# Hybrid encoder layer: the filters' sums of squares and the Hyena column weights on VectorE, the filters' sum one step later, and a final norm that is shared between ScalarE and VectorE

## The chip, the cores and the metric

The kernel runs on one core of one Trainium2 chip. A core has five engines that matter here, each of which works through its own list of instructions in order: TensorE (PE in the profile) multiplies matrices, VectorE (DVE) and ScalarE (ACT) work on tiles element by element, GpSimd (POOL) can do a part of what VectorE does, and SyncE (SP) issues the DMAs. Where an instruction needs what another engine makes, it waits, and all that is behind it on its engine waits too.

The metric is the device time of one execution in microseconds (us). A kernel is judged by the median of several runs.

## What is computed

One layer of a bidirectional encoder over 1024 positions of width 1024, in float32:

```python
x = x + 0.5 * _swiglu(_rmsnorm(x, ffn1_norm), ffn1_w_gu, ffn1_w_down)
h = _rmsnorm(x, mix_norm)
u_hy, u_rw, g_hy, g_rw = jnp.split(h @ w_in, split_at, axis=-1)
y_hy = _hyena_branch(u_hy, ...)
y_rw = _rwkv7_branch(u_rw, ...)
merged = jax.nn.sigmoid(g_hy) * y_hy + jax.nn.sigmoid(g_rw) * y_rw
x = x + merged @ w_out
x = x + 0.5 * _swiglu(_rmsnorm(x, ffn2_norm), ffn2_w_gu, ffn2_w_down)
return _rmsnorm(x, final_norm)
```

Two parts of it matter for the change. The Hyena branch makes its long filters from a small network, scales every filter by its own length, and takes the spectrum of it:

```python
k = jnp.concatenate([fwd, zero, jnp.flip(bwd[1:], axis=0)], axis=0)
k = k * lax.rsqrt(jnp.sum(k * k, axis=0, keepdims=True) + FILTER_EPS)
```

and the last step of the layer is a norm with one weight per feature:

```python
y = xf * lax.rsqrt(jnp.mean(xf * xf, axis=-1, keepdims=True) + RMS_EPS)
return (y * g.astype(jnp.float32)).astype(x.dtype)
```

## The kernel before

**Matmuls.** Every large product is made in three passes: each operand is split into a coarse part (`hi`, a cast, line 33) and the rest (`lo`, a subtraction, line 37), and `mm3` (lines 43 to 45) adds hi·hi, lo·hi and hi·lo in PSUM. Weights come by DMA into a staging tile `w_st`, ScalarE casts `w_hi`, and a second engine subtracts to get `w_lo`. `col_weights` does this for a column block of 128 features; its argument `lo_eng` names the engine of the subtraction, and without it that is GpSimd.

**Stages.** The first FFN, the mixer, the second FFN and the final norm follow each other. A tile framework with a scheduler sets the order of the instructions on each engine ahead of time, by its own estimate of when each is ready; at run time that order is fixed. So an edit at one place can move rows at others.

**The Hyena columns (some 786 to 1066 us).** The loop over `order` (lines 1324 to 1356) takes 12 column blocks of `w_in`. For each, `half` makes two halves of the product (PE, tile `pw`), `ShortConv.take` copies them into `sh_u` and `sh_o` on ScalarE (lines 545 and 546), and `ShortConv.finish` adds the two outer taps of a width-3 convolution with two VectorE instructions of 128x1024 (line 552), transposes the block in eight small matmuls (`hy_tp`, line 558), copies it on ScalarE (`sh_x`, line 559) and stores it.

Between the blocks the loop advances a generator `bg`, `hyena_filters`, which makes four filters. Each filter takes eight taps: a matmul `ps_h` (line 420), an exponential `ex` (422) and a square `sq` (432) on ScalarE, a product `kt` (424) and an even and an odd sum `eo` (438, 440) on VectorE, and on GpSimd the running sum `acc` of the squares (433; the first of the eight is written by ScalarE at line 428, so seven sums are left). After the eighth tap `ac2` (line 499; the trace calls it `ac`) folds `acc`, two sets of small matmuls (501 and 506) add it over the partitions, and a chain over VectorE and ScalarE (503 to 513) makes the scales. Those scales also multiply the convolution's weights `cw` (line 1349). Then `ps_k` (line 448) is the last product of the spectrum, and lines 458 to 525 put its parts together and store them (`kout`). `bg` gives control back at each `yield`, twelve times in a filter; the loop takes it to step 3i before block i, and to the end of the filter that a block needs.

Each engine's list mixes these two kinds of work, the blocks and the filters. PE waits where neither has anything ready.

**After it** the long convolutions run (from about 1066 us), with the next columns of `w_in` beside them: there VectorE already makes the `w_lo` tiles itself (line 1246).

**The end.** In the last group of the second FFN, `down` adds a block of 128 features and 512 positions to `xT` (line 226), `down_weights` makes that block's weights through a chain DMA, ScalarE, GpSimd (tiles `wdst`, `wd_hi`, `wd_lo`), and `Norm.add` squares the block on ScalarE and sums it on VectorE (lines 92 and 93). When the eight blocks of a half (t = 0 or 1) are done, `finish` makes 1/rms and, for each of four row tiles and two halves j of the features, transposes `xT` on PE (`f_ps`, line 1764), scales it on VectorE with the row's 1/rms and with `grow`, a copy of the final norm's weights in all partitions (line 1767), and stores 256 KB (line 1769).

Of the kernel before, what the change touches and what calls it, by code (L numbers as in the profile page):

```python
# [20 lines left out]
P = 128  # L21
# [135 lines left out]
def bcast_row(ap, n=P):  # L157

    return bass.AP(tensor=ap.tensor, offset=ap.offset, ap=[[0, n]] + [list(d) for d in ap.ap])
# [226 lines left out]
def hyena_filters(tc, ctx, I, K, h2, k_dram, scl):  # L386
# [16 lines left out]
    for o in range(2):  # L403
        for hb in range(NHB):
# [13 lines left out]
            def taps(r):  # L418
                ps = psh.tile([P, 2, HB], F32, name="ps_h", tag="ps_h")
                nc.tensor.matmul(ps, h2[:, r, :], w3b, start=True, stop=True)  # L420
                ex = two.tile([P, 2, HB], F32, name="ex")
                nc.scalar.activation(ex, dec, AF.Exp, scale=tneg[:, r : r + 1])
                kt = two.tile([P, 2, HB], F32, name="kt")
                nc.vector.tensor_tensor(kt, ps, ex, ALU.mult)
                if r == 0:
                    nc.vector.memset(kt[0:1, 1, :], 0.0)
                if first[0]:
                    nc.scalar.activation(acc, kt, AF.Square)
                    first[0] = False
                else:  # L430
                    sq = two.tile([P, 2, HB], F32, name="sq")
                    nc.scalar.activation(sq, kt, AF.Square)
                    nc.gpsimd.tensor_tensor(acc, acc, sq, ALU.add)
                return kt

            def even_odd(r, kt):
# [60 lines left out]
            yield  # L497
            ac2 = two.tile([P, HB], F32, name="ac2", bufs=1)
            nc.vector.tensor_tensor(ac2, acc[:, 0], acc[:, 1], ALU.add)
            ps = psh.tile([P, 512], F32, name="ps_h", tag="ps_h")  # L500
            nc.tensor.matmul(ps[0:1, 0:HB], ones, ac2, start=True, stop=True)
            srow = two.tile([1, HB], F32, name="srow", bufs=1)
# [710 lines left out]
def mixer_in(tc, I, K, ident, wp, pw, hl, scl, h2, h2ctx, dr):  # L1213
# [3 lines left out]
    with ExitStack() as ctx:  # L1217
# [100 lines left out]
        with ExitStack() as c2:  # L1318
# [2 lines left out]
            cw = K.cw  # L1321

            order = (8, 9, 10, 11, 0, 1, 2, 3, 4, 5, 6, 7)
            weights = lambda t: col_weights(nc, wp, I["w_in"][:, ts(t, P)], KD)

            w = {t: weights(t) for t in order[0:3]}
            conv = lambda t: ShortConv(nc, two, sx, ptp, ident, cw[:, t])
# [296 lines left out]
def hybrid_layer_kernel(ctx: ExitStack, tc: tile.TileContext, I: dict, out: bass.AP):  # L1624
# [29 lines left out]
    with tc.tile_pool(name="hB", bufs=1) as hp, tc.tile_pool(name="mip", bufs=3, space=PSUM) as pw:  # L1654
# [3 lines left out]
        with ExitStack() as c2:  # L1658
# [3 lines left out]
            with ExitStack() as c3:  # L1662
# [4 lines left out]
                def done(d, t):  # L1667
                    nc.sync.dma_start(x_dram[:, d, ts(t, 512)], xT[:, d, ts(t, 512)])
                    nm.add(xT[:, d, ts(t, 512)], t)
# [58 lines left out]
    with ExitStack() as ctx2:  # L1728
# [20 lines left out]
        with ExitStack() as c3:  # L1749
# [1 line left out]
            pmm = c3.enter_context(tc.tile_pool(name="ffbp", bufs=2, space=PSUM))  # L1751
            nf = Norm(nc, np_, npp, ident, live["ones"], K.norm["final_norm"], "nm2")

            grow = c3.enter_context(tc.tile_pool(name="fg", bufs=1)).tile([P, D], F32, name="f_g")
            nc.sync.dma_start(grow, bcast_row(I["final_norm"]))

            def finish(t):
                r = nf.rstd(t)
                for q in range(4):
                    i = 4 * t + q  # L1760
                    for j in range(KD // 4):
                        ps = pmm.tile([P, 4, P], F32, name="f_ps", tag="pgu", bufs=4)
                        for c in range(4):
                            nc.tensor.transpose(ps[:, c, :], xT[:, 4 * j + c, ts(i, P)], ident)
                        o = np_.tile([P, 512], F32, name="f_o", tag="nm_h") if j else \
                            wp.tile([P, 512], F32, name="f_o", tag="w_st")
                        nc.vector.scalar_tensor_tensor(o, ps.rearrange("p a b -> p (a b)"), r[:, q : q + 1],  # L1767
                                                       grow[:, ts(j, 512)], ALU.mult, ALU.mult)
                        nc.sync.dma_start(out[0, ts(ORDER[i], P), ts(j, 512)], o)

            def pools():
                return (c3.enter_context(tc.tile_pool(name="ffb2", bufs=2)), dn, pmm,
                        lambda: pmm.tile([P, 512], F32, name="pgu", tag="pgu", bufs=4))

            for _ in ffn(nc, pools, wp, xT, live["hl"], I["ffn2_w_gu"], I["ffn2_w_down"],
                         lambda d, t: nf.add(xT[:, d, ts(t, 512)], t), finish):
                pass


# [21 lines left out]
```

## Time and profile before

| | |
|---|---|
| median of 3 runs | 2882.93 us (2874.61 to 2890.05) |
| the profiled execution | 2875.99 us |
| its span | 2874.2 us |
| mean granted clock of TensorE | 0.97 |
| busy: PE, DVE, ACT, POOL | 95%, 43%, 31%, 19% |

The span is the time from the first to the last instruction of the profiled execution; what lies around it is 1.8 us. The profile gives for each engine the busy time, for groups of instructions the mean duration, and for idle time what ended it. A row of the timeline reads: start, duration, engine, line, operation, output and inputs, and in brackets how long the engine had been idle and what released it. The granted clock is the share of full speed that TensorE was allowed to run at.

### The profile page before, as it was taken

To read this page: it belongs to the slowest core of one execution; us is meant where nothing else is said; L and a number is where in the kernel's file an instruction comes from. 1 tells how busy PE (TensorE), PEld (TensorE's weight loads), DVE (VectorE), ACT (ScalarE), POOL (GpSimd) and SP (SyncE) were. 2 spreads that over 40 slices of the span, in tenths; PEclk is the share of its full clock that TensorE was granted. 3 is DMA by queue.
4 is the path that set the end of the run, shared out by engine and by line. 5 is a ranking of instruction groups with operands and counts; after the bars stand their busy time and mean duration, and the time that the engine had idled before them with its cause. 6 is when DMAs were issued, how large, how long until landed. Compare 5 with 4: busy or idle time off the path is not lost. (4 is left out here: it accounts for less than half of the span.)

```text
span 2874.2 us, 46016 instructions
## 1 busy us (share of the span) xinstructions
PE 2723.9 (95%) x19440; PEld 2194.6 (76%) x19440; DVE 1231.8 (43%) x2140; ACT 905.2 (31%) x1515; POOL 550.0 (19%) x351
## 2 busy tenths in 40 slices
PE   8999999999988899989899999898999999999998
PEld 6888888888665667777787877776778888888787
DVE  4111010111647668998765667757541111101114
ACT  5111111111444442334654545532331111111112
POOL 2323233232413210000000000000033232322322
PEclk9999999999988999999999999898999999999999
DMA  5111111111341235553644325457531111111102
GB/s 126 55 48 48 41 55 48 41 52 43 107 148 63 77 127 186 164 169 114 188 118 152 103 88 180 144 171 231 166 88 52 44 52 44 52 44 48 47 27 92
DMA packets 406477, 276.43 MB, mean 96 GB/s; under 512 B 50899, under 2 KB 366879, under 8 KB 405632
## 3 DMA queue, kind: packets, MB, share of 16 engines
q1 hardware_dynamic: 406272, 273.50, 31.5%
q8 instruction: 153, 2.51, 0.4%
q14 instruction: 52, 0.43, 0.0%
HBM read 202.53 MB, written 70.91 MB: 95 GB/s over the span
## 5 line engine op out<-in xcount | busy, mean ns | idle before, releaser
L45 PE MATMUL pw<-hThi,w_lo 128*128 128x512 f32 (+1 forms) x1184 | 472.3, 400 | 15.6 <-DVE w_lo L1246 15.6
L43 PE MATMUL pw<-hThi,w_hi 128*128 128x512 f32 (+1 forms) x1184 | 473.8, 400 | 8.5 <-ACT sh_o L1268 4.4
L44 PE MATMUL pw<-hTlo,w_hi 128*128 128x512 f32 (+1 forms) x1184 | 472.1, 399 | 0.0
L33 ACT CAST w_hi<-w_st 128x1024 fp32r<-128x1024 f32 (+1 forms) x176 | 170.8, 972 | 496.0 <-PE pw L44 187.0
L37 POOL TENSOR_TENSOR w_lo<-w_st,w_hi 128x1024 fp32r<-128x1024 f32 x100 | 240.5, 2405 | 412.3 <-ACT w_hi L33 406.1
L43 PE MATMUL pgu<-hThi,w_hi 128*128 128x512 f32 x704 | 279.0, 396 | 0.8 <-issue 0.8
L44 PE MATMUL pgu<-hTlo,w_hi 128*128 128x512 f32 x704 | 279.1, 396 | 0.2 <-POOL hTlo L37 0.2
L45 PE MATMUL pgu<-hThi,w_lo 128*128 128x512 f32 x704 | 279.1, 397 | 0.0
L43 PE MATMUL pdn<-g_hi,wd_hi 128*128 128x512 f32 x704 | 275.0, 391 | 1.9 <-DVE xT L226 1.9
L44 PE MATMUL pdn<-g_lo,wd_hi 128*128 128x512 f32 x704 | 274.8, 390 | 2.0 <-POOL g_lo L37 2.0
L45 PE MATMUL pdn<-g_hi,wd_lo 128*128 128x512 f32 x704 | 275.0, 391 | 1.4 <-POOL wd_lo L37 1.4
L45 PEld LDWEIGHTS pw<-hThi,w_lo 128*128 128x128 f32 (+1 forms) x1184 | 223.2, 189 | 69.6 <-DVE w_lo L1246 17.8
L43 PEld LDWEIGHTS pw<-hThi,w_hi 128*128 128x128 f32 (+1 forms) x1184 | 223.6, 189 | 63.9 <-ACT sh_o L1268 6.2
L226 DVE SCALAR_TENSOR_TENSOR xT<-pdn,xT 128x512 f32<-128x512 f32 x192 | 132.3, 690 | 314.8 <-PE pdn L45 314.8
L44 PEld LDWEIGHTS pw<-hTlo,w_hi 128*128 128x128 f32 (+1 forms) x1184 | 223.3, 189 | 54.6 <-issue 4.4
L209 DVE TENSOR_TENSOR silu<-silu,pgu 128x512 f32<-128x512 f32 x44 | 30.2, 687 | 449.5 <-PE pgu L45 449.5
L209 DVE TENSOR_TENSOR silu<-silu,pw 128x512 f32<-128x512 f32 x44 | 30.2, 687 | 445.9 <-PE pw L45 445.1
L37 POOL TENSOR_TENSOR wd_lo<-wdst,wd_hi 128x512 fp32r<-128x512 f32 (+1 forms) x112 | 132.4, 1183 | 333.6 <-ACT wd_hi L33 333.6
L37 POOL TENSOR_TENSOR g_lo<-silu,g_hi 128x512 fp32r<-128x512 f32 x88 | 113.5, 1289 | 398.4 <-ACT g_hi L33 398.4
L33 ACT CAST wd_hi<-wdst 128x512 fp32r<-128x512 f32 (+1 forms) x112 | 64.5, 576 | 379.5 <-PE pdn L44 366.9
L37 POOL TENSOR_TENSOR hTlo<-nm_h,hThi 128x512 fp32r<-128x512 f32 x16 | 23.2, 1447 | 740.2 <-ACT hThi L33 740.2
L43 PEld LDWEIGHTS pgu<-hThi,w_hi 128*128 128x128 f32 x704 | 132.5, 188 | 33.2 <-issue 1.2
(316 smaller groups left out, 4461.6 us busy)
## 6 DMA issues: line engine op xcount, KB each, us to landing
w_st<-in_ffn_w_gu SPq DMA_DIRECT2D x88, 512.0 KB, 3.7
w_st<-in_w_in SPq DMA_DIRECT2D x57, 512.0 KB, 3.8
wdst<-in_ffn_w_down SPq DMA_DIRECT2D x64, 256.0 KB, 2.8
wdst<-in_ffn_w_down SPq DMA_DIRECT2D x48, 192.0 KB, 2.5
d_kf<-kout SPq DMA_DIRECT2D x32, 256.0 KB, 2.3
hy_k<-d_kf SPq DMA_DIRECT2D x32, 256.0 KB, 3.3
w_st<-in_w_out SPq DMA_DIRECT2D x16, 512.0 KB, 3.9
d_X<-sh_x SPq DMA_DIRECT2D x12, 512.0 KB, 3.5
```

Source lines behind the costliest of these rows:

```text
L33: nc.scalar.copy(hi, src)
L37: eng.tensor_tensor(lo, src, hi.bitcast(F32), ALU.subtract)
L43: te.matmul(out, lhs[0], rhs[0], start=first, stop=False)
L44: te.matmul(out, lhs[0], rhs[1], start=False, stop=False)
L45: te.matmul(out, lhs[1], rhs[0], start=False, stop=last)
L209: nc.vector.tensor_tensor(sl, sl, pu, ALU.mult)
L226: nc.vector.scalar_tensor_tensor(xa, ps, 0.5, xa, ALU.mult, ALU.add)
```

## The change

Four edits. The sum `acc` of the filters' squares moves from GpSimd to VectorE. A `yield` is put between `ac2` and the matmul that reads it. The `w_lo` tiles of the twelve Hyena column blocks move from GpSimd to VectorE. The final norm's weights are multiplied onto `xT` in place, by ScalarE, as soon as a block has been squared (`done`); the copy of the weights in all partitions goes; the last scaling is left with the row's 1/rms alone, on VectorE for the first half of the features and on ScalarE for the second; and the two halves go into one tile and one store of 512 KB.

```diff
@@ hyena_filters
-                    nc.gpsimd.tensor_tensor(acc, acc, sq, ALU.add)
+                    nc.vector.tensor_tensor(acc, acc, sq, ALU.add)
...
             nc.vector.tensor_tensor(ac2, acc[:, 0], acc[:, 1], ALU.add)
+            yield
             ps = psh.tile([P, 512], F32, name="ps_h", tag="ps_h")
             nc.tensor.matmul(ps[0:1, 0:HB], ones, ac2, start=True, stop=True)
@@ the Hyena columns
-            weights = lambda t: col_weights(nc, wp, I["w_in"][:, ts(t, P)], KD)
+            weights = lambda t: col_weights(nc, wp, I["w_in"][:, ts(t, P)], KD, lo_eng="dve")
@@ the final norm
-            grow = c3.enter_context(tc.tile_pool(name="fg", bufs=1)).tile([P, D], F32, name="f_g")
-            nc.sync.dma_start(grow, bcast_row(I["final_norm"]))
+            fo = c3.enter_context(tc.tile_pool(name="fo", bufs=2))
+
+            def done(d, t):
+
+                x = xT[:, d, ts(t, 512)]
+                nf.add(x, t)
+                nc.scalar.activation(x, x, AF.Copy, scale=nf.g[:, d : d + 1])
 
             def finish(t):
                 r = nf.rstd(t)
                 for q in range(4):
                     i = 4 * t + q
+                    o = fo.tile([P, D], F32, name="f_o") if q % 2 else wp.tile([P, D], F32, name="f_w", tag="w_st")
                     for j in range(KD // 4):
                         ps = pmm.tile([P, 4, P], F32, name="f_ps", tag="pgu", bufs=4)
                         for c in range(4):
                             nc.tensor.transpose(ps[:, c, :], xT[:, 4 * j + c, ts(i, P)], ident)
-                        o = np_.tile([P, 512], F32, name="f_o", tag="nm_h") if j else \
-                            wp.tile([P, 512], F32, name="f_o", tag="w_st")
-                        nc.vector.scalar_tensor_tensor(o, ps.rearrange("p a b -> p (a b)"), r[:, q : q + 1],
-                                                       grow[:, ts(j, 512)], ALU.mult, ALU.mult)
-                        nc.sync.dma_start(out[0, ts(ORDER[i], P), ts(j, 512)], o)
+                        flat = ps.rearrange("p a b -> p (a b)")
+                        if j:
+                            nc.scalar.activation(o[:, ts(j, 512)], flat, AF.Copy, scale=r[:, q : q + 1])
+                        else:
+                            nc.vector.tensor_scalar(o[:, ts(j, 512)], flat, r[:, q : q + 1], None, ALU.mult)
+                    nc.sync.dma_start(out[0, ts(ORDER[i], P), :], o)
...
             for _ in ffn(nc, pools, wp, xT, live["hl"], I["ffn2_w_gu"], I["ffn2_w_down"],
-                         lambda d, t: nf.add(xT[:, d, ts(t, 512)], t), finish):
+                         done, finish):
                 pass
```

The scheduler turns this into new orders. Three places are shown. The first is VectorE's list at the end of the second filter, the last two taps up to `ac`; before:

```order
L424 TENSOR_TENSOR kt<-ps_h,ex 128x512
L438 TENSOR_TENSOR eo<-kt 128x256
L440 TENSOR_TENSOR eo<-kt 128x256
L463 SCALAR_TENSOR_TENSOR cxt<-cxt,ps_k 128x512 x2
L409 SCALAR_TENSOR_TENSOR dec<-dec 128x512
L424 TENSOR_TENSOR kt<-ps_h,ex 128x512
L426 MEMSET kt 1x256
L499 TENSOR_TENSOR ac_5911<-acc 128x256
```

The same place after:

```order
L424 TENSOR_TENSOR kt<-ps_h,ex 128x512
L438 TENSOR_TENSOR eo<-kt 128x256
L440 TENSOR_TENSOR eo<-kt 128x256
L433 TENSOR_TENSOR acc<-acc,sq 128x512
L463 SCALAR_TENSOR_TENSOR cxt<-cxt,ps_k 128x512 x2
L409 SCALAR_TENSOR_TENSOR dec<-dec 128x512
L424 TENSOR_TENSOR kt<-ps_h,ex 128x512
L426 MEMSET kt 1x256
L433 TENSOR_TENSOR acc<-acc,sq 128x512
L499 TENSOR_TENSOR ac_5911<-acc 128x256
```

Each tap has one row more, `acc`, behind its `eo` rows, and it needs the square that ScalarE makes of the same `kt`; GpSimd's list loses those rows, and the `w_lo` rows of the blocks.

The second place is PE's list at the transposes of the second block (`hy_tp`), which wait for the line 552 pair; `pw` rows belong to the next block, `L376` to the small network of the filters. Before:

```order
L43 MATMUL pw<-hThi_119,w_hi 128x512
L376 MATMUL ps_h<-feats,w_5082 64x512
L558 MATMUL hy_tp<-ident,sh_o 128x128 x8
L44 MATMUL pw<-hTlo_120,w_hi 128x512
L45 MATMUL pw<-hThi_119,w_lo 128x512
```

After (the lines behind the new `yield` count one more, so line 558 is 559):

```order
L43 MATMUL pw<-hThi_119,w_hi 128x512
L376 MATMUL ps_h<-feats,w_5082 64x512
L44 MATMUL pw<-hTlo_120,w_hi 128x512
L45 MATMUL pw<-hThi_119,w_lo 128x512
L43 MATMUL pw<-hThi_119,w_hi 128x512
L44 MATMUL pw<-hTlo_120,w_hi 128x512
L45 MATMUL pw<-hThi_119,w_lo 128x512
L559 MATMUL hy_tp<-ident,sh_o 128x128 x8
```

Five `pw` matmuls have moved ahead of the transposes.

The third place is ScalarE's list in the second half (t = 1) of the last FFN group; the blocks of features are counted from 0 to 7. The `CAST` rows make the blocks' weights, the line 92 rows are the squares. Before, from the cast of block 3 on, which the square of block 1 follows:

```order
L33 CAST wd_hi<-wdst 128x384
L92 ACTIVATE nm_sq<-xT 128x512
L33 CAST wd_hi<-wdst 128x384 x2
L92 ACTIVATE nm_sq<-xT 128x512 x2
L33 CAST wd_hi<-wdst 128x384
L92 ACTIVATE nm_sq<-xT 128x512
L33 CAST wd_hi<-wdst 128x384
L92 ACTIVATE nm_sq<-xT 128x512 x3
```

After, from the cast of block 4 on, which the square of block 2 follows:

```order
L33 CAST wd_hi<-wdst 128x384
L92 ACTIVATE nm_sq<-xT 128x512
L1761 ACTIVATE xT<-xT,k_final_norm 128x512
L92 ACTIVATE nm_sq<-xT 128x512
L1761 ACTIVATE xT<-xT,k_final_norm 128x512
L92 ACTIVATE nm_sq<-xT 128x512
L33 CAST wd_hi<-wdst 128x384
L1761 ACTIVATE xT<-xT,k_final_norm 128x512
L33 CAST wd_hi<-wdst 128x384 x2
L92 ACTIVATE nm_sq<-xT 128x512
```

The cast of block 5 stood ahead of the squares of the blocks 2 and 3 before; after, it stands behind the squares of the blocks 2, 3 and 4.

## The prediction

> **What bounds the kernel now.** I read the page first: the busy times, then the forty slices of 72 us for PE and for its granted clock.
>
> ```profile
> PE 2723.9 (95%) x19440; PEld 2194.6 (76%) x19440; DVE 1231.8 (43%) x2140; ACT 905.2 (31%) x1515; POOL 550.0 (19%) x351
> PE   8999999999988899989899999898999999999998
> PEclk9999999999988999999999999898999999999999
> ```
>
> PE is the bound nearly everywhere; what another engine saves pays only where PE waits for it. Slices 11 to 14 show 8s, in the clock too. The table by stage shows what that is (columns: window, length, then the busy time and the instructions of PE, PEld, DVE, ACT and POOL, the granted clock, DMA share, GB/s).
>
> ```profile
> 800.00:850.00 50.00, 41.13 (x165) 30.42 (x165) 29.48 (x38) 24.45 (x34) 10.53 (x4) 0.90 0.28 83
> 900.00:950.00 50.00, 42.11 (x177) 32.06 (x177) 39.33 (x68) 23.00 (x35) 14.56 (x8) 0.93 0.29 93
> 1200.00:1400.00 200.00, 182.38 (x887) 143.90 (x886) 178.11 (x265) 80.24 (x131) 0.96 (x1) 0.98 0.53 157
> 2200.00:2820.00 620.00, 618.98 (x2679) 502.66 (x2678) 80.23 (x117) 102.87 (x148) 178.51 (x111) 1.00 0.15 44
> 2820.00:2874.20 54.20, 44.42 (x223) 36.50 (x221) 34.57 (x59) 19.61 (x34) 15.43 (x15) 0.92 0.36 122
> ```
>
> The second FFN has no room: PE fills 619 of 620 us. The Hyena columns lose 8 to 9 of 50 us, and the end loses 10 of 54. PE's waits between 786 and 1066 us (sum, times, longest):
>
> ```profile
> PE hy_tp L558 <- DVE sh_o L552: 17.3, 10, 3.6
> PE ps_h L501 <- DVE ac L499: 6.9, 4, 4.4
> PE hy_tp L558 <- DVE sh_u L539: 3.6, 1, 3.6
> ```
>
> Of these 27.8 us, 17.3 are the transposes' wait for VectorE's line 552 pair; the longest single wait, 4.4 us, is the first filter's fold waiting for the last sum.
>
> **Why VectorE is late there.** GpSimd does the sums and the `w_lo` tiles, and the two engines stretch each other. The groups of this stage:
>
> ```profile
> L433 POOL TENSOR_TENSOR acc<-acc,sq 128x512 f32<-128x512 f32 x28 | 41.0, 1463 | 97.7 <-ACT sq L432 97.7
> L37 POOL TENSOR_TENSOR w_lo<-w_st,w_hi 128x1024 fp32r<-128x1024 f32 x9 | 22.5, 2499 | 85.3 <-ACT w_hi L33 79.1 <-PE ps_k L448 6.1
> L458 DVE TENSOR_TENSOR cxt<-cxt,ps_k 128x512 f32<-128x512 f32 x16 | 10.0, 678 | 1.4 <-PE ps_k L448 1.4
> L1246 DVE TENSOR_TENSOR w_lo<-w_st,w_hi 128x1024 fp32r<-128x1024 f32 x3 | 3.7, 1220 | 1.6 <-ACT w_hi L1245 1.6
> L552 DVE SCALAR_TENSOR_TENSOR sh_o<-sh_u,k_cw,sh_o 128x1024 f32<-128x1024 f32 x24 | 50.8, 2116 | 29.5 <-ACT sh_o L546 29.4
> L440 DVE TENSOR_TENSOR eo<-kt 128x256 f32<-128x256 f32 x32 | 15.4, 483 | 0.0
> ```
>
> and two collisions in the timeline (start, duration):
>
> ```profile
> 813.15 3.37 POOL L37 TENSOR_TENSOR w_lo<-w_st,w_hi 128x1024 fp32r<-128x1024 f32 x1 [10.29 <-ACT w_hi L33]
> 812.25 6.03 DVE L552 SCALAR_TENSOR_TENSOR sh_o<-sh_u,k_cw,sh_o 128x1024 f32<-128x1024 f32 x2 [5.43 <-ACT sh_o L546]
> 905.15 2.36 POOL L37 TENSOR_TENSOR w_lo<-w_st,w_hi 128x1024 fp32r<-128x1024 f32 x1 [7.04 <-ACT w_hi L33]
> 905.21 2.59 DVE L440 TENSOR_TENSOR eo<-kt 128x256 f32<-128x256 f32 x1
> 910.01 1.49 DVE L525 TENSOR_TENSOR kout<-cxt 128x256 f32<-128x256 f32 x1
> ```
>
> An `eo` that takes 0.48 us on average took 2.59 beside a `w_lo`; a pair that takes 4.2 took 6.03. PE's gaps stand right behind:
>
> ```profile
> 806.89 1.94 PE L558 MATMUL hy_tp<-ident,sh_o 128*128 128x128 f32 x8 [2.62 <-issue]
> 818.42 1.94 PE L558 MATMUL hy_tp<-ident,sh_o 128*128 128x128 f32 x8 [3.55 <-DVE sh_u L539]
> 914.09 1.97 PE L558 MATMUL hy_tp<-ident,sh_o 128*128 128x128 f32 x8 [3.58 <-DVE sh_o L552]
> 948.47 1.07 PE L558 MATMUL hy_tp<-ident,sh_o 128*128 128x128 f32 x8 [2.28 <-DVE sh_o L552]
> 961.65 1.13 PE L448 MATMUL ps_k<-eo,hf_F 128*128 128x256 f32 x4 [1.99 <-DVE eo L438]
> 963.65 1.84 PE L558 MATMUL hy_tp<-ident,sh_o 128*128 128x128 f32 x8 [0.64 <-DVE sh_o L552]
> ```
>
> A gap also costs clock: behind 2.62, 3.55 and 3.58 us the eight transposes take 1.94 to 1.97, behind 2.28 us 1.07. So a gap that falls below some 2.3 us saves about 0.9 more on the transposes.
>
> **The Hyena columns, sum.** VectorE gets 28 sums at 0.68 us (as line 458, same shape) = 19.0, and nine `w_lo` in this window at 1.22 = 11.0: 30 us more. It has room on average (39.33 of 50 in the fullest window shown). Gap by gap, with the new order:
> - 806.89: the pair ran beside a `w_lo` and loses about 0.6 of its excess; the gap falls to 2.0, and the clock gives 0.9: **-1.5**.
> - 818.42: the pair gives back 6.03 - 4.2 = 1.8, five more `pw` matmuls stand ahead of the transposes (a pitch of 0.23 by the second FFN's window, 618.98 us for 2679; so 1.2): 3.0 of 3.55, and 0.9 of clock, and with a bit more overlap I take **-4.1**.
> - 914.09: line 440 gives back 2.1, line 525 1.1, the clock 0.9; a sum and a `w_lo` may now stand ahead, +0.9: **-3.2**.
> - 948.47: the line 552 pair stands ahead of two line 458 rows (1.3) and of no stretched one: **-2.0**.
> - 961.65 and 963.65: 1.99 + 0.64 go, since VectorE's stretched `kout` goes and the transposes move, and 1.84 becomes 1.07: **-3.4**.
> - the first filter's fold (the wait of 4.4): its last sum takes 0.68 in place of 1.46, GpSimd's mean: **-0.7**; the gap stays above 2.3, so its clock stays low.
> - against it, in the chains of taps without `pw` between: VectorE's own row there is
>
> ```profile
> 869.86 0.69 DVE L424 TENSOR_TENSOR kt<-ps_h,ex 128x512 f32<-128x512 f32 x1 [0.49 <-PE ps_h L420]
> 870.64 0.63 ACT L432 ACTIVATE sq<-kt 128x512 f32<-128x512 f32 x1 [0.74 <-DVE kt L424]
> ```
>
> VectorE idles 0.49 us a tap; the sum is 0.68 and hides but for 0.1 to 0.2, over some five taps: **+0.6**.
>
> Together -14.3. The `yield` itself separates nothing: the loop stops at steps 6, 9, the filter's end and 15 as before, and only the second filter is one step shorter at block 5; I cost it at zero, since VectorE and PE have other blocks' work there; if that cover is gone, line 501 waits as before (6.9 us in four waits).
>
> [...]
>
> **Behind and ahead of it.** In the first FFN's last group GpSimd also makes three of those `w_lo`, and PE waits there for `wd_lo`; that goes, **-1.4** (all of this line's idle time):
>
> ```profile
> L45 PE MATMUL pdn<-g_hi,wd_lo 128*128 128x512 f32 x704 | 275.0, 391 | 1.4 <-POOL wd_lo L37 1.4
> 1080.57 3.69 PE L630 MATMUL hy_y<-hy_zz,F 128*128 128x256 f32 x16 [0.29 <-DMA hy_zz<-d_X]
> ```
>
> The long convolution starts (row above) on a load, `hy_zz`, that SP's list now issues behind the first column's store, and VectorE does one `w_lo` (1.22) and two line 1281 rows more before its first product. VectorE is the bound there (178 of 200 us, table above), so what is late stays late: **+2**, bounds 0 and 3.8.
>
> **The end.** Rows of before:
>
> ```profile
> PE pdn L43 <- DVE xT L226: 1.1, 1, 1.1
> 2854.10 0.51 ACT L33 CAST wd_hi<-wdst 128x384 fp32r<-128x384 f32 x1 [0.98 <-PE pdn L44]
> 2854.69 1.02 POOL L37 TENSOR_TENSOR wd_lo<-wdst,wd_hi 128x384 fp32r<-128x384 f32 x1 [2.64 <-ACT wd_hi L33]
> 2858.39 0.68 DVE L226 SCALAR_TENSOR_TENSOR xT<-pdn,xT 128x512 f32<-128x512 f32 x1
> 2866.01 3.65 PE L1764 MATMUL f_ps<-ident,xT 128*128 128x128 f32 x16 [2.33 <-issue]
> L1767 DVE SCALAR_TENSOR_TENSOR f_o<-f_ps,rms_r,f_g x16: 739/742/752, 2844.1 to 2870.1; 128x512 f32<-128x512 f32 x16
> DMA to landing us min/median/max: 2.0/2.1/3.0
> d_X<-sh_x SPq DMA_DIRECT2D x12, 512.0 KB, 3.5
> ```
>
> VectorE's eight scalings of the first half (5.9 us) no longer hold up `xT`: -1.1. ScalarE gets 16 in-place scalings (about 0.63 each, as its square) and eight last scalings. All but the last are beside PE's `pdn`, but the cast of block 5 now stands behind the square of block 4, and so behind that block's `xT`: 0.7 + 0.63 + 0.51, then GpSimd's 1.02 before the third pass, of which PE hides some 0.4. That is a new wait of about 2.5 us; bounds are 0 (if the square is early enough after all) and 2.9 (nothing hidden). At the very end the transposes resume when the first scaling has freed a bank (2866.01), and the span ends 8.2 us later. Two engines now take four scalings each, 4 x 0.7 in place of 8 x 0.74, so PE's 3.65 us for the last 16 transposes sets the pace; then a scaling, 0.7, and a store of 512 KB. That store is bounded by the 2.1 us of the 256 KB stores (row "DMA to landing" of the tile `f_o`) and by the 3.5 of another 512 KB store; between ends so close I take the middle, 2.8: 7.2 us, **-1.0**. Sum: -1.1 + 2.5 - 1.0 = +0.4, say **+0.5**; bounds -2 and +2.5.
>
> **Sum.** -14.3 - 1.4 + 2 + 0.5 = -13.2 us. Against the profiled execution (2875.99, of which the span is 2874.2) that is 2862.8. That execution was 6.9 us under the median shown; on the median it is 2882.93 - 13.2 = **2869.7**, which I round to 2870.
>
> **The rivals.**
> - *The gain is given back (near no change).* The line 552 pair still starts only when ScalarE has written `sh_o`, and PE has no other work for those 4.2 us: the gaps then shrink by the stretches alone (1.8 + 2.1 + 1.1 + 0.6 = 5.6) and the new rows on VectorE cost half of that again. With +3.8 at the long convolution, +2.5 at the end and -1.4: 2 us slower, 2885. For it: the gaps at 948 and later have no collision as large. Against it: the moved transposes. That the `yield` does nothing belongs here.
> - *VectorE becomes the late engine (slower).* In its list each `acc` waits for a square that ScalarE makes behind other work; all behind it, `eo` and the line 552 pairs too, waits with it. It decides where the wait and the 0.68 exceed VectorE's 0.49 us of idle time a tap. Priced: 28 x 0.19 = 5.3, plus nine `w_lo` ahead of what PE waits for, 11.0, plus 2.5 behind (as the sum, and no relief): 2883 + 19 = 2902. Against it: VectorE is idle 11 of 50 us even in its fullest window, and gets back the stretches.
> - *More is gained.* If most gaps fall under 2.3 us, the matmuls behind them run at full clock too, not only the transposes: the granted clock of 0.90 and 0.93 in two windows of 50 us is 8.5 us of lost rate, of which the terms above take 3.6. With -5 more and the end at -2: 2870 - 7.5 = 2862.
>
> **How the numbers follow.** Forecast 0.46 (2865 to 2877), given back 0.26, more gained 0.16, slower 0.12. 0.5% is about what a measurement of this kernel can tell from no change, 14.4 us: under 2868.5 is faster. That takes the third rival and two fifths of the forecast, whose middle lies just above it: 0.34. Slower, over 2897, is most of the second rival: 0.10. The rest, 0.56, is no change. The range leaves out the slower rival above and the lower edge of the larger gain, and takes the bounds of the unknown terms: 2856 to 2888.
>
> **What would show it.** In the profile after: GpSimd has no rows from 786 to 1066 us but two `hTlo`; line 433 on VectorE takes 0.68 and no `eo` over 0.6; the gaps before the transposes of the second block (818) and at 914 fall below 1 us; the three rows of PE's waits fall from 27.8 us to about 17; the wait of block 5 in the last half is 2 to 3 us. I am wrong if VectorE's waits for `sq` add up to more than 5 us, or if the transposes wait as long as before though nothing is stretched.

## The result and the profile after

| | before | after |
|---|---|---|
| median | 2882.46 us (2874.61 to 2890.05, 6 runs) | 2861.41 us (2854.11 to 2868.68, 6 runs) |
| ratio | | 0.9929, 95% interval 0.9911 to 0.9948 |
| profiled execution, its span | 2875.99, 2874.2 us | 2864.08, 2862.1 us |

The change is faster by 21 us, 0.7%. The two profiled executions differ by 12 us only: that of before lay 6.5 us under its median, that of after 2.7 us above. A second comparison of the same two kernels, told below, gave 0.9947 (0.9927 to 0.9967), that is 15 us. So what the traces show stage by stage has to explain 12 to 21 us.

The page of the kernel after, the same three lines as were shown of before:

```profile
PE 2719.7 (95%) x19440; PEld 2190.6 (77%) x19440; DVE 1248.4 (44%) x2172; ACT 920.5 (32%) x1539; POOL 480.7 (17%) x311
PE   8999999999988999999998988898999999999998
PEclk9999999999999999999999999898999999999999
```

The shares moved by a point or two. But in the Hyena columns the clock's two 8s (slices 12 and 13) are gone, and PE has two 8s where it had three. The table by stage (window, length, busy time and instructions of PE, PEld, DVE, ACT, POOL, granted clock, DMA share, GB/s):

```profile
800.00:850.00 50.00, 44.29 (x189) 32.50 (x188) 33.03 (x44) 25.26 (x36) 0.00 (x0) 0.97 0.38 112
900.00:950.00 50.00, 45.88 (x201) 34.53 (x200) 43.74 (x81) 23.96 (x36) 0.00 (x0) 1.00 0.36 114
1200.00:1400.00 200.00, 184.49 (x1150) 145.27 (x1148) 173.32 (x269) 80.81 (x135) 1.01 (x1) 0.98 0.52 157
2807.90:2862.10 54.20, 43.97 (x221) 35.60 (x219) 28.94 (x50) 35.02 (x58) 15.52 (x15) 0.96 0.35 122
```

In the two windows of the Hyena columns GpSimd is silent, VectorE works 4 us more in each window of 50, and PE does 24 instructions more in the same time, at a clock of 0.97 and 1.00 where 0.90 and 0.93 were granted. The end loses 10 us of 54, as before. PE's waits from 786 to 1066 us, all of them:

```profile
PE hy_tp L559 <- DVE sh_o L553: 12.8, 11, 1.7
PE pw L43 <- ACT sh_o L547: 3.9, 1, 3.9
PE ps_h L502 <- DVE ac L499: 3.5, 1, 3.5
PE ps_h L420 <- DVE kt L424: 2.5, 4, 0.8
PE hy_tp L559 <- issue: 2.1, 1, 2.1
```

Two more make 0.7. The three kinds of wait shown of before, 27.8 us, are 16.3 now. The gaps themselves, before the first, second, sixth and eighth block's transposes:

```profile
806.03 1.28 PE L559 MATMUL hy_tp<-ident,sh_o 128*128 128x128 f32 x8 [2.11 <-issue]
816.00 1.07 PE L559 MATMUL hy_tp<-ident,sh_o 128*128 128x128 f32 x8 [0.60 <-DVE sh_o L553]
903.28 1.09 PE L559 MATMUL hy_tp<-ident,sh_o 128*128 128x128 f32 x8 [1.71 <-DVE sh_o L553]
948.75 1.06 PE L559 MATMUL hy_tp<-ident,sh_o 128*128 128x128 f32 x8 [0.43 <-DVE sh_o L553]
```

The gap of 3.55 us is 0.60, that of 3.58 is 1.71, and 1.99 + 0.64 became 0.57 (before a line 420 matmul) + 0.43; behind all but the first the eight transposes run at full rate (1.06 to 1.09 us, at a granted clock of 1.00; the first took 1.28). On VectorE (groups from 786 to 1066 us):

```profile
L433 DVE TENSOR_TENSOR acc<-acc,sq 128x512 f32<-128x512 f32 x28 | 19.3, 688 | 3.7 <-ACT sq L432 3.7
L37 DVE TENSOR_TENSOR w_lo<-w_st,w_hi 128x1024 fp32r<-128x1024 f32 x9 | 11.0, 1223 | 17.4 <-ACT w_hi L33 17.1
L440 DVE TENSOR_TENSOR eo<-kt 128x256 f32<-128x256 f32 x32 | 13.3, 415 | 0.0
L553 DVE SCALAR_TENSOR_TENSOR sh_o<-sh_u,k_cw,sh_o 128x1024 f32<-128x1024 f32 x24 | 48.9, 2037 | 12.1 <-ACT sh_o L547 12.0
```

The new work is 30.3 us; the `eo` rows fell from 483 to 415 ns, the line 552 rows (now 553) from 2116 to 2037. VectorE waits 3.7 us for squares.

What the columns gained shows best at points that both kernels pass. These are starts in the traces (us); a fold is the first matmul of line 501 (502 after) of a filter:

| | before | after | difference |
|---|---|---|---|
| first transposes | 806.9 | 806.0 | -0.9 |
| fold of filter 1 | 884.2 | 878.0 | -6.2 |
| fold of filter 2 | 934.8 | 924.8 | -10.0 |
| fold of filter 3 | 988.1 | 972.3 | -15.8 |
| fold of filter 4 | 1038.0 | 1019.4 | -18.6 |
| first product of the long convolution | 1080.6 | 1066.8 | -13.8 |
| first `psA<-rw_xt,rw_a` of the RWKV scan | 1410.8 | 1393.3 | -17.5 |
| last gate matmul of the second FFN | 2819.3 | 2806.6 | -12.7 |
| end of the span | 2874.2 | 2862.1 | -12.1 |

(The long convolution of before starts at 1080.6, and not at about 1066, where its columns end.) So 18.6 us are won in the columns and 4.8 of them are gone again when the long convolution starts. Between the last transposes and that start 88 `pw` matmuls stand in PE's list and not 63; the 25 more are 5.8 us at the pitch of 0.23 us, so that work is done earlier. Another part is a wait, in PE's timeline and SP's list of DMA issues (SPq) of after:

```profile
1066.76 7.20 PE L631 MATMUL hy_y<-hy_zz,F 128*128 128x256 f32 x32 [2.51 <-issue]
1052.36 0.33 SPq L1382 DMA_DIRECT2D F<-in_c_fwd  x1
1053.48 0.52 SPq L1314 DMA_DIRECT2D d_r<-sh_o  x1
1054.56 0.84 SPq L1317 DMA_DIRECT2D d_r<-sh_v  x1
1055.45 4.58 SPq L743 DMA_DIRECT2D hy_zz<-d_X  x1
```

The load of `hy_zz` stands behind two stores and takes 4.58 us to issue, and PE waits 2.51 us. In before it stood right behind the load of `F` and took 0.58, and the wait was 0.29:

```profile
1071.51 0.33 SPq L1381 DMA_DIRECT2D F<-in_c_fwd  x1
1071.89 0.58 SPq L742 DMA_DIRECT2D hy_zz<-d_X  x1
```

The end, in the second half of the last FFN group (PE, then ScalarE):

```profile
2841.30 0.50 PE L43 MATMUL pdn<-g_hi,wd_hi 128*128 128x512 f32 x1 [1.35 <-ACT wd_hi L33]
2842.49 0.50 PE L45 MATMUL pdn<-g_hi,wd_lo 128*128 128x512 f32 x1 [0.46 <-POOL wd_lo L37]
2854.41 3.41 PE L1771 MATMUL f_ps<-ident,xT 128*128 128x128 f32 x16 [1.99 <-ACT f_w L1774]
2840.22 0.63 ACT L92 ACTIVATE nm_sq<-xT 128x512 f32<-128x512 f32 x1 [0.65 <-DVE xT L226]
2840.75 0.49 ACT L33 CAST wd_hi<-wdst 128x384 fp32r<-128x384 f32 x1
```

The cast of block 5 waits for the square of block 4, and PE for the cast and then for the `wd_lo` that GpSimd makes: 1.81 us, where the wait for `xT`, 1.1, is gone. From the last gate matmul to the end it takes 55.5 us, against 54.9 before.

### The profile page after: what moved, and what is told of

The parts are those of the page before. It is cut to its first block, busy times and chain, and to the rows that moved or that the text cites. A ratio compares the mean times of both kernels' runs of the same rounds, so it can differ in the third digit from the quotient of the medians.

```text
span 2862.1 us, 45943 instructions
## 1 busy us (share of the span) xinstructions
PE 2719.7 (95%) x19440; PEld 2190.6 (77%) x19440; DVE 1248.4 (44%) x2172; ACT 920.5 (32%) x1539; POOL 480.7 (17%) x311
## 3 DMA queue, kind: packets, MB, share of 16 engines
q8 instruction: 153, 2.51, 0.4%
## 5 line engine op out<-in xcount | busy, mean ns | idle before, releaser
L44 PEld LDWEIGHTS pw<-hTlo,w_hi 128*128 128x128 f32 (+1 forms) x1184 | 223.7, 189 | 54.9 <-issue 4.4
L37 POOL TENSOR_TENSOR w_lo<-w_st,w_hi 128x1024 fp32r<-128x1024 f32 x88 | 210.8, 2395 | 316.9 <-ACT w_hi L33 316.8
L45 PEld LDWEIGHTS pgu<-hThi,w_lo 128*128 128x128 f32 x704 | 132.5, 188 | 32.1
```

Source lines behind the costliest of these rows:

```text
L37: eng.tensor_tensor(lo, src, hi.bitcast(F32), ALU.subtract)
L44: te.matmul(out, lhs[0], rhs[1], start=False, stop=False)
L45: te.matmul(out, lhs[1], rhs[0], start=False, stop=last)
```

## The experiments

**Theory:** the gain is made in the Hyena columns, because GpSimd no longer stretches VectorE's instructions; the end gives and takes; the yield does nothing. **Rivals:** the final norm brings a part; the yield, or the new order rather than the quiet GpSimd, makes the gain; one of the two moves makes all of it.

### The parts that stand outside the columns

*no_tail.* The first three edits alone; the final norm stays as before.

> All of the change but the final norm, which stays as before. Theory (the gain is made in the Hyena columns, the end gives and takes about 0.5 us): as fast as the full change within 3 us, ratio to before 0.992 to 0.994; in its trace the last matmul of the second FFN comes as early as in the full change, and what follows takes 55 us as before. Rival (a good part of the 21 us is the final norm's): ratio 0.996 or more.

2866.16 us, ratio 0.9948 (0.9928 to 0.9967). The long convolution starts at 1067.8, and from the last gate matmul to the end it takes 54.7 us. A little less was gained than I expected, but as much as the full change has on its second comparison: the final norm is no part of the gain that can be seen.

*tail_only.* The final norm's edit alone.

> The final norm's part of the change alone. Theory: ratio 0.999 to 1.001; in the last half a new wait of PE for the cast of block 5, 1 to 3 us, in place of the 1.1 us wait for xT. Rival (the end brings what the profiled pair does not show): ratio 0.997 or less, 8 us or more.

2882.86 us, ratio 1.0006 (0.9990 to 1.0023). In its trace the wait for the cast is 1.4 us and the stretch from the last gate matmul 55.9. The theory holds. The traces say a little more than the times: in the six with the new end that ScalarE shares, this stretch takes 55.5 to 58.5 us, in the seven with the old one 54.4 to 54.9. So the edit costs 0.6 us or more.

*no_yield.*

```diff
             nc.vector.tensor_tensor(ac2, acc[:, 0], acc[:, 1], ALU.add)
-            yield
```

> The full change without the added yield. Theory (the yield separates nothing): the full change's time within 3 us, ratio 0.992 to 0.994, transposes and folds wait as in the full change, about 23 us in the stage. Rival (the later sum gives PE work ahead of the fold, and that is part of the gain): ratio 0.995 or more, and the waits for the fold (line 502) grow to over 5 us.

2867.99 us, ratio 0.9960 (0.9945 to 0.9975). Its trace agrees with the theory: the long convolution starts at 1066.7 (1066.8 with the yield), the fold waits 3.4 us, the transposes 13.8 and 2.1. The ratio lies on the rival's side, but its interval overlaps both of the full change's. What the yield is worth, between nothing and some 9 us (0.9960 against the first comparison's 0.9929), stays open; none of it can be seen up to the long convolution.

*full_again.* The full change, unchanged, on the chip of the next three runs.

> The full change once more, beside its parts on one chip. Theory: what the first trace of it shows (the Hyena columns end 22 us and the long convolution starts 14 us earlier, the rest moves by 3 us or less either way) makes 13 to 17 us, so the median lies 13 to 17 us under before (ratio 0.994 to 0.9955), and the 21 us of the first comparison was partly luck of its six runs. Rival (something behind the columns gains as well): 19 us or more, ratio 0.9935 or less.

2865.44 us against 2878.78, ratio 0.9947 (0.9927 to 0.9967). The theory's value, though the interval doesn't exclude the rival's. Its columns repeat those of the first trace (folds at 877.6, 924.3, 971.8 and 1019.0, long convolution at 1066.1).

### Which move makes the gain

*acc_only.*

```diff
-                    nc.gpsimd.tensor_tensor(acc, acc, sq, ALU.add)
+                    nc.vector.tensor_tensor(acc, acc, sq, ALU.add)
```

> Only the sum of the squares on VectorE; the w_lo tiles stay on GpSimd, no yield, final norm as before. Theory (both moves share the gain): ratio 0.996 to 0.998, the long convolution starts 5 to 9 us earlier than before; the fold of the first filter waits about 3.5 us and not 4.4; the transposes at 806 and 818 us keep their waits of 2.6 and 3.5 us. Rival (the sums are the whole gain): ratio 0.9955 or less.

2877.75 us, ratio 0.9989 (0.9974 to 1.0005): hardly anything. The waits at the first fold (3.4 us) and at the first two transposes (2.6 and 3.3) are as expected; the long convolution starts only 1.4 us earlier.

*wlo_only.*

```diff
-            weights = lambda t: col_weights(nc, wp, I["w_in"][:, ts(t, P)], KD)
+            weights = lambda t: col_weights(nc, wp, I["w_in"][:, ts(t, P)], KD, lo_eng="dve")
```

> Only the w_lo tiles of the Hyena columns on VectorE; the sums stay on GpSimd. Theory: ratio 0.996 to 0.998, the wait before the transposes at 818 us (3.6) is gone, no VectorE pair of line 552 over 4.6 us, the long convolution starts 5 to 9 us earlier. Rival (the w_lo tiles are the whole gain): ratio 0.9955 or less.

2862.92 us, ratio 0.9942 (0.9920 to 0.9965): as much as the full change. Here the rival was right and my theory of equal shares wrong. One line 552 row still takes 3.00 us for 2.0, beside a sum on GpSimd, which I hadn't expected either. The points from the traces say where the moves differ:

| start (us) | before | acc_only | wlo_only | full_again |
|---|---|---|---|---|
| fold of filter 1 | 884.2 | 884.3 | 877.9 | 877.6 |
| fold of filter 2 | 934.8 | 932.9 | 927.0 | 924.3 |
| fold of filter 3 | 988.1 | 982.3 | 977.1 | 971.8 |
| fold of filter 4 | 1038.0 | 1031.0 | 1024.3 | 1019.0 |
| long convolution | 1080.6 | 1079.2 | 1067.2 | 1066.1 |

Inside the columns the two moves nearly add up: 7.0 and 13.7 us at the fourth fold, 19.0 together. But from there to the long convolution it takes 42.6 us before, 42.9 in wlo_only, and 48.2 and 47.1 where the sums are on VectorE. The sums' gain is given back in that stretch: there the load of `hy_zz` stands behind the two stores and 88 `pw` matmuls stand ahead, in wlo_only the load is right behind `F` and there are 60. It doesn't come back later: the RWKV scan starts at 1410.4 us in acc_only, and at 1410.8 in before.

### Whether it is the company of GpSimd or the new order

*pool_beside.* The full change; GpSimd adds each square to itself, into a tile of its own. The lists of the other engines stay as they are, row for row.

```diff
                     nc.vector.tensor_tensor(acc, acc, sq, ALU.add)
+                    idle = two.tile([P, 2, HB], F32, name="idle", bufs=1)
+                    nc.gpsimd.tensor_tensor(idle, sq, sq, ALU.add)
```

> The full change, and GpSimd adds each square to itself into a tile that nothing reads (28 additions of 128x512; the output does not depend on them). The lists of the other four engines stay row for row those of the full change, so only the company on GpSimd returns. Theory (GpSimd's rows stretch VectorE's): some VectorE rows beside them take 1 to 2 us where 0.4 is usual, VectorE is busy 4 to 8 us longer in the stage, and the kernel is 3 to 8 us slower than the full change (ratio 0.994 to 0.996). Rival (the new order makes the gain, not the quiet GpSimd): VectorE's medians unchanged, time within 1 us of the full change, ratio 0.992 to 0.9935.

2875.65 us, ratio 0.9977 (0.9959 to 0.9996): by the medians more than half of the gain is lost by work that nobody waits for, though the interval overlaps that of full_again. The groups of that kernel from 786 to 1066 us, and the tile `kout` (min/median/max in ns):

```profile
L433 DVE TENSOR_TENSOR acc<-acc,sq 128x512 f32<-128x512 f32 x28 | 20.9, 748 | 3.7 <-ACT sq L432 3.7
L433 POOL TENSOR_TENSOR idle<-sq 128x512 f32<-128x512 f32 x28 | 43.0, 1537 | 192.5 <-ACT sq L432 192.5
L525 DVE TENSOR_TENSOR kout<-cxt x24: 411/420/1267, 902.6 to 1055.7; 128x256 f32<-128x256 f32 x24
```

A `kout` that takes 0.42 us takes up to 1.27 again, and VectorE is busy 5.0 us more from 780 to 1066 (217.2 against 212.2). The folds come 0.9, 4.9, 6.0 and 7.2 us later than in the full change, the long convolution 6.1. The order is the same, so these 6 to 7 us come from GpSimd's company; that is about what acc_only won at the fourth fold (7.0). The 7.7 us that remain at the long convolution's start against before (1072.9 against 1080.6) this run doesn't divide between the quiet of GpSimd's `w_lo` rows and the new order. By the ratios (0.9977 against full_again's 0.9947) it is some 9 us; what is behind the long convolution differs by as much from trace to trace (last section).

*wlo_beside.* As wlo_only, and GpSimd adds each `w_hi` to itself into a tile that nothing reads.

```diff
+            idle = sx.tile([P, KD, P], F32, name="idle", bufs=1)
+            beside = lambda w: (nc.gpsimd.tensor_tensor(idle, w[0].bitcast(F32), w[0].bitcast(F32), ALU.add), w)[1]
-            weights = lambda t: col_weights(nc, wp, I["w_in"][:, ts(t, P)], KD, lo_eng="dve")
+            weights = lambda t: beside(col_weights(nc, wp, I["w_in"][:, ts(t, P)], KD, lo_eng="dve"))
```

> As wlo_only (only the w_lo tiles of the Hyena columns on VectorE, ratio 0.9942), and GpSimd adds each w_hi to itself into a tile that nothing reads: 12 additions of 128x1024, so GpSimd runs a tile of the old size at about the old times, but no one waits for it (the output does not depend on it). VectorE's list differs from wlo_only's in the place of two rows, PE's in that of some pw rows. Theory (the gain of the w_lo move is that a long GpSimd instruction no longer stretches the VectorE rows beside it): line 552 pairs of 5 to 6 us return, the second fold and the long convolution come 5 to 11 us later than in wlo_only, ratio 0.996 to 0.9985. Rival (the gain is that the tile itself is ready sooner, 1.2 us after its cast instead of 2.4, and that PE's list is another): the folds within 2 us of wlo_only's, ratio 0.995 or less.

2878.20 us, ratio 0.9991 (0.9976 to 1.0005): in time all of the gain is lost. First VectorE's rows in wlo_only (a pair of line 552, and a `w_lo` between two such rows):

```profile
801.08 4.08 DVE L552 SCALAR_TENSOR_TENSOR sh_o<-sh_u,k_cw,sh_o 128x1024 f32<-128x1024 f32 x2 [0.44 <-ACT sh_o L546]
812.64 1.21 DVE L37 TENSOR_TENSOR w_lo<-w_st,w_hi 128x1024 fp32r<-128x1024 f32 x1
```

and the same rows in wlo_beside, each under its neighbour on GpSimd, with a wait of PE that followed:

```profile
798.38 2.87 POOL L1324 TENSOR_TENSOR idle<-w_hi 128x1024 f32<-128x1024 f32 x1 [3.22 <-ACT w_hi L33]
799.95 5.10 DVE L552 SCALAR_TENSOR_TENSOR sh_o<-sh_u,k_cw,sh_o 128x1024 f32<-128x1024 f32 x2 [0.45 <-ACT sh_o L546]
811.53 2.87 POOL L1324 TENSOR_TENSOR idle<-w_hi 128x1024 f32<-128x1024 f32 x1 [10.28 <-ACT w_hi L33]
812.56 2.92 DVE L37 TENSOR_TENSOR w_lo<-w_st,w_hi 128x1024 fp32r<-128x1024 f32 x1
844.51 1.37 PE L558 MATMUL hy_tp<-ident,sh_o 128*128 128x128 f32 x8 [3.21 <-DVE sh_o L552]
```

4.08 became 5.10, and 1.21 became 2.92. The folds are at 884.5, 935.4, 986.7 and 1034.2, 6.5 to 9.9 us later than in wlo_only, and the long convolution at 1076.0: 9.9 of the 13.7 us at the fourth fold are lost, and 8.8 of 13.4 there. A tile that is ready sooner is therefore at most a small part of the gain: six of the nine end 1.26 us behind their cast, as in wlo_only, and most of the gain is gone. The other three end 1.7 to 5.5 us later than there, behind VectorE's rows that are stretched or stand elsewhere. So two things are not separated: the additions also stand ahead of the sums in GpSimd's own list and hold their `w_hi` tiles longer, and a few rows of the other engines' lists have moved.

Taken together: at the fourth fold GpSimd's idle additions take back 7.2 us of the full change's 18.6 (the sums') and 9.9 of wlo_only's 13.7 (the tiles'). Most of what the columns won is the quiet; some 2 to 4 us may be the new order or the sooner tile.

### The end, and what was given back

*gain_dve.* The full change, with the weights multiplied onto `xT` by VectorE.

```diff
-                nc.scalar.activation(x, x, AF.Copy, scale=nf.g[:, d : d + 1])
+                nc.vector.tensor_scalar(x, x, nf.g[:, d : d + 1], None, ALU.mult)
```

> The full change, but the final norm's weights are multiplied onto xT by VectorE and not by ScalarE. Theory (the new wait in the last half comes from ScalarE's list, where the cast of block 5 stands behind the square of block 4): the wait for that cast is gone or under 1 us, and the stretch from the last gate matmul of the second FFN to the end is 53.5 to 54.5 us against the full change's 55.5. Rival (the wait comes from the weights' load, which is issued behind four stores): the wait stays at 1.3 to 1.8 us, the stretch at 55 us or more. In the whole time 1 to 2 us, which the comparison cannot tell.

2871.97 us, ratio 0.9967 (0.9952 to 0.9982). Half right: the wait for the cast is gone, so it did come from ScalarE's list. But the stretch from the last gate matmul is 59.7 us and not 54. PE's waits at its end, and one of VectorE's new rows:

```profile
PE f_ps L1771 <- DVE xT L1761: 3.9, 2, 2.3
PE pdn L43 <- DVE xT L226: 0.8, 1, 0.8
2851.41 1.22 DVE L1761 TENSOR_SCALAR xT<-xT,k_final_norm 128x512 f32<-128x512 f32 x1
```

PE's transposes of the half before stand ahead of `pdn` in its list and wait for VectorE's multiplications, and those, 0.47 us alone, take 1.22 beside GpSimd's `wd_lo`. In this trace the multiplication was better placed on ScalarE.

*zz_early.* no_tail, with the first load of the long convolution issued right behind that of `F`.

```diff
             nc.sync.dma_start(F, I["c_fwd"])
+            z0 = hy2.tile([P, RT, HF], F32, name="hy_zz", bufs=1)
+            nc.sync.dma_start(z0, dr["X"][2][:, :, ts(0, HF)])
...
-        z = two.tile([P, RT, HF], F32, name="hy_zz", bufs=1)
-        nc.sync.dma_start(z, X[2][:, :, ts(hb, HF)])
+        z = two.tile([P, RT, HF], F32, name="hy_zz", bufs=1) if hb else z0
+        if hb:
+            nc.sync.dma_start(z, X[2][:, :, ts(hb, HF)])
```

> The full change without its final norm, and the long convolution's first load (hy_zz) is issued right behind the load of F, as it was before the change, and not behind two stores. Theory (the sums' gain of some 5 us in the columns is given back because the long convolution starts on that load): PE's wait at its first product falls from 2.2 us to under 1, that product comes 3 to 6 us earlier than 1067 us, and the median falls by 2 to 6 us against the full change (ratio 0.9925 to 0.994). Rival (VectorE bounds the long convolution, so an earlier start is lost inside it): the first product comes earlier, but the RWKV part starts within 2 us of the full change's 1393 to 1398 us, ratio 0.9945 to 0.996.

2858.62 us, ratio 0.9930 (0.9909 to 0.9950).

*acc_zz* and *zz_full*: the same edit on acc_only and on the full change.

> As acc_only (only the sums on VectorE, ratio 0.9989), with the long convolution's first load issued right behind the load of F. Theory (the sums gain some 7 us in the columns, and the late load gives 5 of them back): the fourth fold at about 1031 us as in acc_only, the first product of the long convolution at 1073 to 1076 us and not 1079, ratio 0.9965 to 0.9985. Rival (the load's place is not what delays it): that product at 1078 us or later, ratio 0.9985 or more.

> The whole change, final norm included, with that load issued early. Theory (4 to 5 us are gained at the long convolution's start and kept): first product at 1061 to 1063 us, ratio 0.9915 to 0.9935, the best of the versions beside zz_early. Rival (what zz_early showed was a lucky set of runs): ratio 0.9945 or more.

acc_zz: 2875.08 us, ratio 0.9978 (0.9962 to 0.9993). zz_full: 2865.67 us, ratio 0.9950 (0.9931 to 0.9969). The first product in acc_only, acc_zz and zz_early, in this order:

```profile
1079.21 6.03 PE L630 MATMUL hy_y<-hy_zz,F 128*128 128x256 f32 x19 [3.26 <-issue]
```

```profile
1072.50 7.35 PE L630 MATMUL hy_y<-hy_zz,F 128*128 128x256 f32 x32 [1.89 <-DVE w_lo L1247]
```

```profile
1062.23 9.04 PE L631 MATMUL hy_y<-hy_zz,F 128*128 128x256 f32 x32 [1.81 <-DVE w_lo L1248]
```

The early load brings the long convolution 6.7 us forward in acc_zz and some 4 to 5.5 in zz_early and zz_full (1062.2 and 1062.4; without it 1066.1 to 1067.8), and the RWKV scan still starts earlier: at 1402.4 against 1410.4, and at 1390.2 and 1390.4 against 1393.3 to 1396.4. The theory holds up to there, and the rival of a loss inside the long convolution isn't borne out. But the wait didn't fall under 1 us: PE waits 1.3 to 1.9 us for a `w_lo` on VectorE instead. The larger part is PE's list, which the scheduler changed with the load: 74 `pw` matmuls stand ahead of the start and not 88, which is 3.2 us at 0.23 each. In the whole time it is not settled: zz_early's median is the lowest of all, zz_full's ratio is the one that the rival named, and the intervals overlap with the full change's. In zz_full's trace the end takes 58.5 us for 55.5, with the lists of the full change and a granted clock of 0.84 over its last 54.2 us where the full change had 0.96. That the edit beats the full change is shown in the traces up to the scan, not by the times.

## Why the prediction came out as it did

It said 2870 us, a gain of 13.2; the first comparison gave 2861.4 us, a gain of 21, the second 13 by its medians and 15 by its ratio. A gain of more than 14.4 us had a chance of 0.34. By its own steps:

- **The columns, -14.3.** Right in place and, for most of it, in cause. Laid against the folds: the terms up to the first fold, with the first FFN's, were -7.7, and -6.2 was measured; -3.2 between the first and second fold, measured -3.8; -5.4 up to the third, measured -5.8; nothing up to the fourth, measured -2.8. The +0.6 of the taps lies in no one stretch. Together that is -15.7, and -18.6 was measured. The term that was missing is the last stretch, where two gaps before transposes (1.83 and 1.76 us) became 1.39 and 1.13, and the fold's wait of 0.78 went; that is 1.9 of the 2.8.
- **The clock.** I took it at 0.9 us for each of four sets of transposes and put the matmuls behind them into the rival "more is gained". The granted clock rose from 0.90 to 0.97 and from 0.93 to 1.00 in the two windows: 3.5 us each. That is 7 us in all, where my terms had 3.6 and the rival 8.6: the rival's mechanism was at work, at nearly its size. What failed here is the reading that only the transposes pay, and only behind more than some 2.3 us: in the columns of before and after a fall of the clock lasts 3.41 us or a multiple (10.2 us at half rate from 800 to 850 us in before, 3.4 after), and a gap of 1.71 us was enough for one (last section).
- **VectorE has room: right.** 30.3 us more work, of which the taps show: PE's waits for `kt` at line 420 rose from 0.9 to 2.5 us, and VectorE's for squares are 3.7, under the 5 that I had named as the limit. The slower rival never came near. The signs named for this held: `eo` takes 0.43 us at most, the three rows of waits are 16.3 us for about 17, the gap at 818 is 0.60.
- **The 914 gap below 1 us: wrong.** It fell to 1.71.
- **The yield at zero:** up to the long convolution right; beyond it not settled.
- **The first FFN, -1.4:** half of it. Two waits of 0.35 us for `wd_lo` stay in that stage; the first transposes come 0.9 us earlier in all.
- **The long convolution's start, +2, bounds 0 and 3.8: mis-sized.** 4.8 us were given back. The late load was seen in the order, but I had argued from the wait alone; `hy_zz` takes 4.58 us to issue behind the two stores, and PE's list has 25 `pw` matmuls more ahead of the start. Neither was in my sum. With the load issued early some 4 to 5.5 us come back, 3.2 of them by that list. I had also called VectorE the bound of the stage at 178 of 200 us; in the same row PE is busy for 182.
- **Up to the long convolution's start, -13.7 in sum, and -13.8 measured: luck.** The columns were 2.9 us better than I said and the start 2.8 us worse, and the two misses cancel.
- **The end, +0.5:** 0.6 in this pair (55.5 against 54.9 us). In its parts: the wait for `xT` is gone; the new wait is 1.81 where I had 2.5, under the 2 to 3 that I had named as a sign; from the resumed transposes to the end it takes 7.7 us (8.2 before), where I had 7.2. The last stores land after 2.6 to 3.3 us, where I had taken 2.8. That the sum met the pair so closely is in part luck, since the same end took up to 58.5 us in other traces.
- **What it didn't ask:** the share of each edit. Gap by gap I had mixed the two moves. The `w_lo` tiles alone give the whole gain in time; the sums win 7 us in the columns, which come back out at the long convolution's start.

What stays open is the difference between 13 and 21 us. Up to the scan the traces show 14.4 and 17.5 (1396.3 and 1393.3 against 1410.8); from the scan's start to the end it then takes 1468.8 and 1469.6 us, 5 to 6 more than the 1463.4 of before. Over all fourteen traces that stretch takes 1460 to 1481 us, and what sets it was not tried.

## What to carry to other kernels

An engine at 19% that is seldom waited for can still be what a busy engine is held up by. Here an `eo` of 0.42 us took up to 2.59 beside GpSimd's row: look for rows that take several times their median, and for what the neighbour ran just then; an idle copy of the neighbour's work, with the order kept, tells whether the company or the order costs. When a stage gets faster, look at what starts the next one: here a load behind two stores, and the matmuls that the scheduler then put ahead, took back what one of the two moves had won. Check a sum at points along the way, too: two misses of nearly 3 us cancelled here. And what a comparison can tell has a floor. Points that both kernels pass tell more: between the two traces of the full change they differ by 0.7 us at most up to the long convolution (and by 3 at the scan), where the ratios' intervals are 11 us wide.

## What the runs showed of the hardware

**A stretched `eo` or `kout` row of VectorE ends 0.3 us behind GpSimd's row.** In rows of before that were shown, GpSimd's `w_lo` ends at 905.15 + 2.36 = 907.51 and the `eo` beside it at 905.21 + 2.59 = 907.80; the sum that GpSimd makes next,

```profile
907.80 3.41 POOL L433 TENSOR_TENSOR acc<-acc,sq 128x512 f32<-128x512 f32 x1 [0.30 <-ACT sq L432]
```

ends at 911.21, and the `kout` beside it at 910.01 + 1.49 = 911.50. Both times VectorE's row ends 0.3 us after GpSimd's, and so do the other six `eo` and `kout` rows that were stretched in this stage. It goes the other way too: this sum, 1.27 us alone, began 0.08 us after a line 552 row and took 3.41. Which rows are hit shows in the tiles of before (min/median/max in ns):

```profile
L424 DVE TENSOR_TENSOR kt<-ps_h,ex x32: 672/690/693, 860.5 to 1034.1; 128x512 f32<-128x512 f32 x32
L440 DVE TENSOR_TENSOR eo<-kt x32: 406/416/2587, 861.5 to 1041.2; 128x256 f32<-128x256 f32 x32
L458 DVE TENSOR_TENSOR cxt<-cxt,ps_k x16: 673/678/689, 871.3 to 1027.0; 128x512 f32<-128x512 f32 x16
```

Of these, the rows with an operand in PSUM (`ps_h`, `ps_k`) never took over 0.69 us, though 11 of the 32 and 10 of the 16 ran beside a GpSimd row; 128x256 rows with both operands in SBUF took up to 2.59, and `gain_dve`'s multiplication, with one tensor in SBUF, 1.22 for 0.47. What makes the difference no run here shows.

**The clock behind a gap is not decided by the gap's length alone.** Eight transposes behind a gap of 2.1 us took 1.28 us in the full change; behind 2.28, 1.07 (before); behind 2.62, 1.94 (before); behind 3.21, 1.37 (wlo_beside). The granted clock in the traces shows more. In before and after it changes only on one grid of steps of 3.41 us: the falls at 806.75, 816.99 and 912.57 us of before are 3 and 28 steps apart. Over the columns (786 to 1066 us) of all fourteen traces each of the 60 falls to half rate came after a step in which PE was busy for 53% or less, and the 984 steps that full rate followed had it busy for 45% or more (in before and after alone 9 falls, at 44% or less, and 146 steps, at 46% or more). So in these traces a gap cost clock where it left one step about half empty. Two gaps of 1.71 us before the same transposes show it, in no_tail and in the full change (the transposes, then the steps with PE's busy time and the clock):

```profile
903.03 1.90 PE L559 MATMUL hy_tp<-ident,sh_o 128*128 128x128 f32 x8 [1.71 <-DVE sh_o L553]
899.75:903.16 3.41, 1.70 (x7) 0.88 (x6) 3.41 (x5) 0.62 (x2) 0.00 (x0) 1.00 0.23 82
903.16:906.57 3.41, 3.41 (x13) 3.02 (x14) 3.39 (x11) 1.79 (x4) 0.00 (x0) 0.50 0.20 77
```

```profile
898.90:902.31 3.41, 2.67 (x11) 1.62 (x9) 3.41 (x4) 1.72 (x4) 0.00 (x0) 1.00 0.35 129
902.31:905.73 3.42, 2.45 (x15) 2.19 (x16) 3.42 (x8) 1.08 (x2) 0.00 (x0) 1.00 0.38 142
```

In no_tail the gap lies within one step, which PE fills to half, and the next runs at half rate; in the full change it lies across two, no step falls under 70%, and the eight transposes (903.28, shown above) take 1.09 us for 1.90.

**One kernel's runs spread by 7 to 29 us**, and the RWKV scan, whose matmuls no run changes, seems to take part in it: from its first `psA<-rw_xt,rw_a` to its last `psA<-rw_BT,rw_t` it took 503.5 us in wlo_only's trace, 508.0 in before's and 517.3 in pool_beside's, at a mean granted clock from 1420 to 1900 us of 0.94, 0.92 and 0.91. These are three kernels; the two traces of the full change differ by 5.2 us in it (507.4 and 512.6, at 0.94 and 0.92). Why the clock differs there was not tried.
